# Sliding-window attention in sixteen fixed rounds: TensorE's order written out by hand

## The chip, the cores and the metric

The kernel runs on one core of one Trainium2 chip. The metric is the device time of one launch in microseconds (us), median of several runs; lower is better.

## What the reference computes

Two layers over 512 tokens of width 1024, everything in float32. Layer 0 mixes tokens with a stick-breaking attention beside a gated recurrence; layer 1 ("the second mixer") is a sliding-window attention with 16 query heads that share 4 key-value heads, a learned sink and a relative bias. Both layers follow it with a convolutional gated feed-forward net and a gate on a per-layer embedding. Only the second mixer is touched by the change:

```python
def mixer_c(h, w_in, q_norm, k_norm, sinks, rel_bias, w_out):
    q, k, v = jnp.split(h @ w_in, [1024, 1280], axis=-1)
    q = rmsnorm(q.reshape(B, S, 16, 64), q_norm)
    k = rmsnorm(k.reshape(B, S, 4, 64), k_norm)
    ...
    # per block of 128 queries, against the 256 keys of its own and the previous block
    logits = einsum('bqhgd,bkhd->bhgqk', q, k) * 64 ** -0.5 + bias   # masked to the band
    m = max(max(logits), sink)
    e = exp(logits - m)
    w = e / (sum(e) + exp(sink - m))
    o = einsum('bhgqk,bkhd->bqhgd', w, v)
    return o.reshape(B, S, 1024) @ w_out
```

Behind the mixer comes `h = h + mixer_c(...)`, then the feed-forward net, then `h = h + sigmoid(rmsnorm(h) @ ple_gate) * (p @ ple_proj)`.

## The kernel before

**Arithmetic.** Activations lie transposed: a tile holds 128 features by 512 tokens. A large product takes each operand apart into a rounded high part and a remainder (`whi`, `wlo` for weights, `xhi`, `xlo` for activations), and `mm3` (L180) adds three matmuls of 512 columns. `weights` (L155) loads 128 x 1024 floats on SP's queue into one of two `wraw` buffers and gives chunks of 512 columns: ScalarE casts `whi` (L168), VectorE subtracts `wlo` (L169), seven buffers of each. `fm_steps` (L187) is one output tile of 128 features, two chunks of twelve matmuls into `psfm`, with a `yield` behind each chunk; `fm` (L198) runs it through. `lead` (L273) does two output tiles at once while their inputs still arrive. `tm` (L206) makes the value projection with tokens on the partitions (`pstm`). The attention itself is plain float32: scores, transposes and values are single matmuls of whole float32 operands; in the trace one such matmul of scores, values or norm is recorded as two passes, and a transpose as one.

**Staging of the second mixer.** `mixer_c` (L696) handles two heads at a time: `jt` counts eight pairs of query heads. Per `jt` it needs the projection of 128 query features (`project`, L718: `psfm`, then `y` on VectorE and its square `sqc` on ScalarE), its norm (`normed`, L727: a matmul `pn` with a block of ones, then Ln and Exp on ScalarE and the product `qn` on VectorE), and two units of attention, `n0` = 0 and 2, each of two query blocks. A unit is
- `scores` (L748): q times k into `pl` (four matmuls, the two heads on rows 0 to 63 and 64 to 127 of the array), bias and maximum on VectorE (L766), four Exp on ScalarE, the sum and reciprocal, and four scalings of `lg` on VectorE (L783);
- `values` (L786): transposes of `lg` into `pt` (six or eight), a copy to `wt` by ScalarE for one head and by VectorE for the other, and the products with `vt` into `poc` (six or eight matmuls, the two heads on columns 0 to 63 and 64 to 127).

After the second unit `split_tile` makes the output projection's input. At the end, `fill` (the `embed` of layer 1, L879, into `pspp`) computes the embedding term that the last stage needs; it doesn't depend on the mixer.

**Who sets the order.** No line of `mixer_c` fixes it: the framework takes the instructions in the order of the program as priorities, and puts on each engine's queue, one after another, the first one whose inputs and buffers it reckons to be there. So the order on TensorE mixes projections, scores, transposes and values, down to single matmuls. Once built, each engine's queue runs strictly in its order. PSUM has two buffers of two banks (tag `z`: `pl`, `pt`, `pstm`), two single banks `mm` (`psfm`, `pn`, `pspp`) and two single banks `hg` (`poc`).

Of the kernel before, what the change touches and what calls it, by code (L numbers as in the profile page):

```python
# [9 lines left out]
F32 = mybir.dt.float32  # L10
F32R = mybir.dt.float32r
U8 = mybir.dt.uint8
AF = mybir.ActivationFunctionType
ALU = mybir.AluOpType

P = 128
# [7 lines left out]
NT = T // P  # L24
# [11 lines left out]
V_KN = V_QN + 1  # L36
# [6 lines left out]
LEAD = (2, 2)  # L43
# [7 lines left out]
class Kern:  # L51
# [642 lines left out]
        return bias  # L694

    def mixer_c(self, st, bias, fill):  # L696
        nc, A = self.nc, self.A
        xs = st["xs"]
        W = A["w_c"]
        with ExitStack() as ctx:  # L700
            kp = self.pool("c_keep", 1, ctx=ctx)
            tp = self.pool("c_tmp", 2, ctx=ctx)
            first = self.lead([W[8], W[9]], st)
            pss = [t[:, a, :] for t in (self.zpair("pstm"), self.zpair("pstm")) for a in range(2)]
            tok = self.tm(A["w_cv"], xs, 256, pss)
            for _ in range(LEAD[0]):
                next(tok)
            self.norm(st, "hg")
            rstd = st["rstd"]
            for _ in range(LEAD[1]):  # L710
                next(tok)
            self.columns(st, "hg")
            sink = kp.tile([P, 16], F32, name="sink")
            nc.gpsimd.dma_start(out=sink, in_=A["sinks"].partition_broadcast(P))
            gq = kp.tile([P, 1], F32, name="gq")
            nc.vector.tensor_scalar(out=gq, in0=self.v(V_QN), scalar1=0.125, scalar2=None, op0=ALU.mult)

            def project(wi):  # L718

                ps = first.pop(0) if first else self.fm(W[wi], xs)  # L720
                y = tp.tile([P, T], F32, tag="y", name="y")
                nc.vector.tensor_tensor(out=y, in0=ps, in1=rstd, op=ALU.mult)
                sq = tp.tile([P, T], F32, tag="sqc", name="sqc")
                nc.scalar.activation(sq, y, AF.Square)
                return y, sq

            def normed(y, sq, gain, tag, bufs):  # L727

                pn = self.bank("pn")
                nc.tensor.matmul(pn, self.blk, sq, start=True, stop=True)  # L730
                self.act(SET_EL, sq, pn, AF.Ln, scale=1.0 / 64, bias=self.eps)
                self.act(SET_EL, sq, sq, AF.Exp, scale=-0.5)
                o = kp.tile([P, T], F32, tag=tag, name=tag, bufs=bufs)
                nc.vector.scalar_tensor_tensor(out=o, in0=y, scalar=gain, in1=sq, op0=ALU.mult, op1=ALU.mult)
                return o

            kn = [project(8 + i) for i in range(2)]
            kn = [normed(*x, self.v(V_KN), "kn", 2) for x in kn]
            vt = []
            for _ in tok:  # L740
                pass
            for i in range(NT):
                t = kp.tile([P, 256], F32, tag="vt", name="vt", bufs=4)
                nc.scalar.activation(t, pss[i][:, 0:256], AF.Identity, scale=st["rcol"][:, i:i + 1])
                vt.append(t)
            os_, qs, pos, pend = [], {}, {}, []

            def scores(jt, n0):  # L748

# [33 lines left out]
                        nc.vector.tensor_scalar(out=lg[a][:, i, :wid[i]], in0=lg[a][:, i, :wid[i]], scalar1=dn[:, c:c + 1], scalar2=None, op0=ALU.mult)  # L783
                return jt, n0, wid, lg

            def values(jt, n0, wid, lg):  # L786
                if n0 == 0:
                    pos[jt] = self.bank("poc", "hg")
                po = pos[jt]
                wts = []  # L790
                pts = self.zpair("pt").rearrange("p a (i k) -> p a i k", i=2)
                for a in range(2):
                    for i in range(2):
                        for b in range(wid[i] // P):
                            nc.tensor.transpose(out=pts[:, a, i, b * P:(b + 1) * P], in_=lg[a][:, i, b * P:(b + 1) * P], identity=self.ident)  # L795
                for a in range(2):
                    pt = pts[:, a, :, :]
                    wt = tp.tile([P, 2, 256], F32, tag="wt", name="wt", bufs=4)
                    cp = nc.vector.tensor_copy if a else nc.scalar.copy
                    if wid[0] == wid[1]:  # L800
                        cp(out=wt, in_=pt)
                    else:
                        for i in range(2):
                            cp(out=wt[:, i, :wid[i]], in_=pt[:, i, :wid[i]])
                    wts.append(wt)
                for i in range(2):
                    n = n0 + i
                    for b in range(wid[i] // P):
                        j = n + 1 - wid[i] // P + b
                        for a in range(2):  # L810
                            g = 2 * (jt // 4) + a
                            nc.tensor.matmul(po[a * 64:a * 64 + 64, n * P:(n + 1) * P], vt[j][:, g * 64:(g + 1) * 64],  # L812
                                             wts[a][:, i, b * P:(b + 1) * P], start=(n == 0), stop=False, skip_group_check=True)
                if n0 == 2:
                    self.dump_ps(f"oc{jt}", po, tp)
                    os_.append(self.split_tile(self.xa, po))

            two = [project(jt) for jt in range(2)]
            for jt in range(2):
                qs[jt] = normed(*two[jt], gq, "qn", 3)  # L820
            for jt in range(8):
                for n0 in (0, 2):
                    pend.append(scores(jt, n0))
                    if jt + 2 < 8:
                        if n0 == 0:
                            nxt = project(jt + 2)
                        else:
                            qs[jt + 2] = normed(*nxt, gq, "qn", 3)
                    if len(pend) > 2:
                        values(*pend.pop(0))  # L830
            for x in pend:
                values(*x)
            fill()
            return os_


# [42 lines left out]
    def embed(self, L, pp, pr):  # L879

        nc, A = self.nc, self.A
        pt = [(hi, lo) for _, hi, lo in self.weights(A["pT"][L], 2 * T)]
        for c0 in range(2):
            for d0, hi, lo in self.weights(A[f"w_pp{L}"][c0], 1024):
                for j in range(2):
                    ps = self.bank("pspp")
                    for k in range(2):
                        sl = slice(j * 256 + k * P, j * 256 + (k + 1) * P)
                        self.mm3(ps, (hi[:, sl], lo[:, sl]), pt[k], k == 0, k == 1)
                    o = pp.tile([P, T], F32, tag="pr", name="pr", bufs=KT)  # L890
                    nc.scalar.copy(out=o, in_=ps)
                    pr.append(o)

    def ple(self, L, st, nxt, pp, pr):
        nc, A = self.nc, self.A
        xs = st["xs"]
        with ExitStack() as ctx:
            tp = self.pool(f"p_tmp{L}", 2, ctx=ctx)
            if pr:
                first = self.lead(A[f"w_pg{L}"][0:2], st)  # L900
            else:
                first = []
                self.embed(L, pp, pr)
            self.norm(st)
            rstd = st["rstd"]
            for m in range(KT):
                end = nxt is None and m == KT - 1
                ch = list(self.weights(A[f"w_pg{L}"][m], DM)) if end else None
                for c in (slice(0, 256), slice(256, T)) if end else (slice(0, T),):
                    if end:  # L910
                        ps = self.bank("psfm")[:, c]
                        for k in range(KT):
                            s = slice(k % 4 * P, k % 4 * P + P)
                            self.mm3(ps, [w[:, s] for w in ch[k // 4][1:]], [x[:, c] for x in xs[k]], k == 0, k == KT - 1)
                    else:
                        ps = first.pop(0) if first else self.fm(A[f"w_pg{L}"][m], xs)
                    g = tp.tile([P, T], F32, tag="pg", name="pg")[:, c]
                    nc.vector.tensor_tensor(out=g, in0=ps, in1=rstd[:, c], op=ALU.mult)  # L918
                    self.act(SET_SG, g, g, AF.Sigmoid)
                    nc.vector.tensor_tensor(out=g, in0=g, in1=pr[m][:, c], op=ALU.mult)  # L920
                    nc.vector.tensor_tensor(out=self.h[m][:, c], in0=self.h[m][:, c], in1=g, op=ALU.add)
                    if nxt is None:
                        nc.sync.dma_start(out=A["out"][m * P:(m + 1) * P, c], in_=self.h[m][:, c])
                if nxt is not None:
                    self.feed(self.xb, m, V_MIX + 8, nxt)
# [118 lines left out]
```

## Time and profile before

| | |
|---|---|
| median of 3 runs | 1335.3 us (1330.41 to 1336.96) |
| the profiled execution's own time | 1332.75 us |
| its span, first to last instruction | 1330.9 us |
| busy share of the span: TensorE matmul, VectorE, ScalarE, GpSimd | 99%, 65%, 51%, 2% |
| mean granted TensorE clock | 0.996 of full speed |
| the second mixer from its third projection to the start of the output projection | 762.72 to 878.35 us of the span |

The busy share of TensorE overstates its work, because consecutive matmuls overlap in the records: the time that one takes from the next is read from start to start.

### The profile page before, as it was taken

To read this page: it belongs to the slowest core of one execution; us is meant where nothing else is said; L and a number is where in the kernel's file an instruction comes from. 1 tells how busy PE (TensorE), PEld (TensorE's weight loads), DVE (VectorE), ACT (ScalarE), POOL (GpSimd) and SP (SyncE) were. 2 spreads that over 40 slices of the span, in tenths; PEclk is the share of its full clock that TensorE was granted. 3 is DMA by queue.
4 is the path that set the end of the run, shared out by engine and by line. 5 is a ranking of instruction groups with operands and counts; after the bars stand their busy time and mean duration, and the time that the engine had idled before them with its cause. 6 is when DMAs were issued, how large, how long until landed. Compare 5 with 4: busy or idle time off the path is not lost.

```text
span 1330.9 us, 16861 instructions
## 1 busy us (share of the span) xinstructions
PE 1311.9 (99%) x6162; PEld 1057.5 (79%) x6162; DVE 861.7 (65%) x1609; ACT 684.7 (51%) x1224; POOL 23.1 (2%) x116
## 2 busy tenths in 40 slices
PE   9999999999999999999998999999999999999998
PEld 7787767788888888888887866678888888888887
DVE  6557876766777347775458377665777536776555
ACT  6566876845544234454355465654644324444341
POOL 2000000000000000000010000000000000000000
PEclk8999999999999999999999999999999999999999
DMA  6321111133332333232364210023332333332232
GB/s 203 112 64 49 58 40 47 48 95 95 96 98 88 99 111 95 95 92 87 93 158 124 95 49 32 22 91 95 96 96 88 100 101 106 96 96 87 89 110 79
DMA packets 37283, 118.95 MB, mean 89 GB/s; under 512 B 4432, under 2 KB 8832, under 8 KB 37200
## 3 DMA queue, kind: packets, MB, share of 16 engines
q1 hardware_dynamic: 35856, 114.31, 27.8%
q0 software_dynamic: 1200, 3.55, 1.3%
q8 instruction: 48, 0.79, 0.2%
q14 instruction: 35, 0.29, 0.1%
q10 hardware_dynamic: 144, 0.02, 0.0%
HBM read 115.37 MB, written 2.49 MB: 89 GB/s over the span
## 4 chain that ended last, share of the span: by engine, by line
PE 89%; DVE 4%; DMA 3%; ACT 2%; issue 1%; SPq 0%; ACTq 0%; DVEq 0%
PE psfm L183 25%; PE psfm L185 24%; PE psfm L184 24%; DMA wraw<-w_pg 2%; PE pl L760 2%; PE poc L812 2%; PE pstm L217 1%; PE pstm L218 1%; PE pstm L216 1%; PE pt L795 1%; PE poa L591 1%; DVE wlo L169 1%; ACT sl L71 1%; PE pn L730 1%; PE psz L574 1%
## 5 line engine op out<-in xcount | busy, mean ns | idle before, releaser
L168 ACT CAST whi<-wraw 128x512 fp32r<-128x512 f32 (+1 forms) x428 | 260.6, 612 | 425.4 <-PE psfm L184 324.8
L183 PE MATMUL psfm<-xhi,whi 128*128 128x512 f32 (+1 forms) x1200 | 472.0, 394 | 4.9 <-DVE pg L918 3.8
L184 PE MATMUL psfm<-xlo,whi 128*128 128x512 f32 (+1 forms) x1200 | 468.4, 391 | 0.8 <-DVE xlo L234 0.8
L185 PE MATMUL psfm<-xhi,wlo 128*128 128x512 f32 (+1 forms) x1200 | 468.6, 391 | 0.1
L169 DVE TENSOR_TENSOR wlo<-wraw,whi 128x512 fp32r<-128x512 f32 (+1 forms) x428 | 287.5, 676 | 175.9 <-ACT whi L168 155.2
L183 PEld LDWEIGHTS psfm<-xhi,whi 128*128 128x128 f32 x1200 | 226.6, 189 | 52.7 <-issue 5.5
L184 PEld LDWEIGHTS psfm<-xlo,whi 128*128 128x128 f32 x1200 | 226.6, 189 | 49.0 <-DVE xlo L234 2.1
L185 PEld LDWEIGHTS psfm<-xhi,wlo 128*128 128x128 f32 x1200 | 226.4, 189 | 47.9 <-issue 1.3
L185 PE MATMUL psfm<-ghi,wlo 128*128 128x512 f32 x352 | 137.0, 389 | 0.0
L184 PE MATMUL psfm<-glo,whi 128*128 128x512 f32 x352 | 137.0, 389 | 0.0
L183 PE MATMUL psfm<-ghi,whi 128*128 128x512 f32 x352 | 137.0, 389 | 0.0
L852 DVE TENSOR_TENSOR u<-psfm,rstd 128x512 f32<-128x512 f32 x88 | 60.7, 691 | 69.3 <-PE psfm L185 64.5
L856 DVE SCALAR_TENSOR_TENSOR cy<-u,vec,cy 128x512 f32<-128x512 f32 x88 | 66.0, 751 | 35.6 <-ACT cy L855 35.4
L855 ACT ACTIVATE cy<-u,vec 128x512 f32<-128x512 f32 x88 | 71.7, 816 | 33.4 <-DVE u L852 33.3
L184 PEld LDWEIGHTS psfm<-glo,whi 128*128 128x128 f32 x352 | 66.1, 188 | 13.8
L185 PEld LDWEIGHTS psfm<-ghi,wlo 128*128 128x128 f32 x352 | 66.1, 188 | 13.6
L183 PEld LDWEIGHTS psfm<-ghi,whi 128*128 128x128 f32 x352 | 66.1, 188 | 13.6
L289 DVE TENSOR_TENSOR h<-h,psfm 128x512 f32<-128x512 f32 x48 | 33.0, 687 | 59.9 <-PE psfm L185 59.9
L857 DVE SCALAR_TENSOR_TENSOR cy<-u,vec,cy 128x512 f32<-128x512 f32 x88 | 65.9, 751 | 2.9
L869 ACT CAST ghi<-cy 128x512 fp32r<-128x512 f32 x44 | 27.3, 621 | 39.6 <-DVE cy L866 39.6
L233 ACT ACTIVATE xhi<-h,gains 128x512 fp32r<-128x512 f32 x48 | 34.6, 723 | 19.5 <-DVE h L289 10.2
L234 DVE SCALAR_TENSOR_TENSOR xlo<-h,gains,xhi 128x512 fp32r<-128x512 f32 x48 | 36.3, 756 | 8.7 <-ACT xhi L233 8.4
(217 smaller groups left out, 1306.1 us busy)
## 6 DMA issues: line engine op xcount, KB each, us to landing
wraw<-w_up SPq DMA_DIRECT2D x88, 512.0 KB, 3.5
wraw<-w_dn SPq DMA_DIRECT2D x32, 512.0 KB, 3.6
wraw<-w_ab SPq DMA_DIRECT2D x18, 512.0 KB, 3.5
wraw<-w_pg SPq DMA_DIRECT2D x16, 512.0 KB, 3.6
wraw<-w_dn SPq DMA_DIRECT2D x32, 192.0 KB, 2.4
wraw<-w_c SPq DMA_DIRECT2D x10, 512.0 KB, 3.5
wraw<-w_abo SPq DMA_DIRECT2D x8, 512.0 KB, 3.5
wraw<-w_co SPq DMA_DIRECT2D x8, 512.0 KB, 3.5
```

Of the source, the lines that this page charges most:

```text
L168: nc.scalar.copy(out=hi[:, :d1 - d0], in_=r)
L169: nc.vector.tensor_tensor(out=lo[:, :d1 - d0], in0=r, in1=hi[:, :d1 - d0], op=ALU.subtract)
L183: t.matmul(ps, w[0], x[0], start=first, stop=False)
L184: t.matmul(ps, w[0], x[1], start=False, stop=False)
L185: t.matmul(ps, w[1], x[0], start=False, stop=last)
L233: nc.scalar.activation(hi, h, AF.Identity, scale=g)
L234: nc.vector.scalar_tensor_tensor(out=lo, in0=h, scalar=g, in1=hi, op0=ALU.mult, op1=ALU.subtract)
L289: self.nc.vector.tensor_tensor(out=self.h[m], in0=self.h[m], in1=ps, op=ALU.add)
L852: nc.vector.tensor_tensor(out=u[:, 2:], in0=ps, in1=rstd, op=ALU.mult)
L855: nc.scalar.activation(y, u[:, 2:], AF.Identity, scale=w[2], bias=w[3])
L856: nc.vector.scalar_tensor_tensor(out=y, in0=u[:, 1:T + 1], scalar=w[1], in1=y, op0=ALU.mult, op1=ALU.add)
L857: nc.vector.scalar_tensor_tensor(out=y, in0=u[:, 0:T], scalar=w[0], in1=y, op0=ALU.mult, op1=ALU.add)
```

## The change

TensorE's instructions of the second mixer are issued in the order of the program (`tc.manual_schedule` for that engine alone). The order of the other engines stays the framework's, and so does the place of TensorE instructions from outside the region among those of the region. The program's order is rewritten: `values` is cut into `turned` (transposes and copies) and `values` (products); the projections of `jt` 2 to 7 and the embedding become a generator `dense` that gives half a projection, or a quarter of the embedding, at a time: twelve matmuls either way. Sixteen rounds follow, one per unit `u`: scores of unit u, values of unit u - 3, one step of `dense`, in odd rounds from 3 to 13 the norm `pn` of the head pair whose scores open the next round, transposes of unit u - 2. The loads of `sinks` and the scaled gain `gq` move ahead of `lead`; the key norms move behind the first query projection. No matmul, copy or load is added or left out.

```diff
             first = self.lead([W[8], W[9]], st)
-            kn = [project(8 + i) for i in range(2)]
-            kn = [normed(*x, self.v(V_KN), "kn", 2) for x in kn]
...
-            for jt in range(8):
-                for n0 in (0, 2):
-                    pend.append(scores(jt, n0))
-                    if jt + 2 < 8:
-                        if n0 == 0:
-                            nxt = project(jt + 2)
-                        else:
-                            qs[jt + 2] = normed(*nxt, gq, "qn", 3)
-                    if len(pend) > 2:
-                        values(*pend.pop(0))
-            for x in pend:
-                values(*x)
-            fill()
+            def dense():
+                for jt in range(2, 8):
+                    steps = project(jt, got)
+                    next(steps)
+                    yield
+                    for _ in steps:
+                        pass
+                    yield
+                yield from fill()
+
+            with tc.manual_schedule(engines={mybir.EngineType.PE}):
...
+                for _ in project(0, got):
+                    pass
+                for i in range(2):
+                    kn[i] = normed(*got[8 + i], self.v(V_KN), "kn", 2)
+                for _ in project(1, got):
+                    pass
+                qs[0] = normed(*got[0], gq, "qn", 3)
+                d = dense()
+                next(d)
+                qs[1] = normed(*got[1], gq, "qn", 3)
+                scored, keyed = [], []
+                for u in range(16):
+                    scored.append(scores(u // 2, u % 2 * 2))
+                    if len(keyed):
+                        values(*keyed.pop(0))
+                    next(d, None)
+                    if u % 2 and 2 <= u // 2 + 1 < 8:
+                        qs[u // 2 + 1] = normed(*got[u // 2 + 1], gq, "qn", 3)
+                    if len(scored) > 2:
+                        keyed.append(turned(*scored.pop(0)))
+                for x in scored:
+                    next(d, None)
+                    keyed.append(turned(*x))
+                    if len(keyed) > 1:
+                        values(*keyed.pop(0))
+                for x in keyed:
+                    values(*x)
+                for _ in d:
+                    pass
```

`turned` holds the transposes and copies of the old `values` word for word; `embed` gains a `yield` behind each twelve matmuls, and layer 0 runs it through as before.

## Rows read from the trace of the kernel before

**Rows 1.** Windows: the mixer, two double rounds; busy us by engine, clock, DMA share, GB/s
```profile
762.72:878.35 115.63, 114.17 (x674) 76.84 (x673) 84.04 (x320) 72.50 (x224) 0.16 (x3) 1.00 0.12 38
810.21:824.61 14.40, 14.40 (x86) 9.90 (x85) 11.04 (x44) 8.71 (x28) 0.00 (x0) 1.00 0.07 29
824.61:839.01 14.40, 14.40 (x86) 9.91 (x85) 10.60 (x41) 8.61 (x28) 0.00 (x0) 1.00 0.11 38
```

**Rows 2.** Timeline of TensorE, part of a double round: start, us, instruction, count
```profile
810.21 0.81 PE L795 MATMUL pt<-cst,lg 128*128 128x128 f32 x6
810.95 0.70 PE L760 MATMUL pl<-kn,qn 64*128 64x256 f32 x2
811.58 0.43 PE L812 MATMUL poc<-wt,vt 128*64 128x128 f32 x2
811.94 0.70 PE L760 MATMUL pl<-kn,qn 64*128 64x256 f32 x4
812.57 0.87 PE L812 MATMUL poc<-wt,vt 128*64 128x128 f32 x10
813.37 0.70 PE L760 MATMUL pl<-kn,qn 64*128 64x256 f32 x2
814.00 1.13 PE L730 MATMUL pn<-sqc,cst 128*128 128x512 f32 x2
814.96 1.04 PE L795 MATMUL pt<-cst,lg 128*128 128x128 f32 x8
```

**Rows 3.** Timeline of TensorE: blocks that stand whole, and what follows them
```profile
793.20 0.50 PE L183 MATMUL psfm<-xhi,whi 128*128 128x512 f32 x1
...
796.06 0.82 PE L795 MATMUL pt<-cst,lg 128*128 128x128 f32 x6
...
797.79 1.13 PE L760 MATMUL pl<-kn,qn 64*128 64x256 f32 x6
798.85 0.44 PE L812 MATMUL poc<-wt,vt 128*64 128x128 f32 x4
...
801.88 0.93 PE L760 MATMUL pl<-kn,qn 64*128 64x128 f32 x8
802.74 0.50 PE L183 MATMUL psfm<-xhi,whi 128*128 128x512 f32 x1
```

**Rows 4.** Timeline of all engines: from a norm's matmul to the scores behind it
```profile
815.16 0.69 ACT L71 ACTIVATE sqc<-pn,eps 128x512 f32<-128x512 f32 x1 [2.82 <-PE pn L730]
815.88 0.63 ACT L71 ACTIVATE sqc<-sqc 128x512 f32<-128x512 f32 x1
816.55 0.75 DVE L734 SCALAR_TENSOR_TENSOR qn<-y,gq,sqc 128x512 f32<-128x512 f32 x1 [0.33 <-ACT sqc L71]
817.40 0.70 PE L760 MATMUL pl<-kn,qn 64*128 64x256 f32 x2
```

**Rows 5.** Groups by line and form, 810.21 to 839.01 us: busy us, mean ns
```profile
L71 ACT ACTIVATE lg<-lg,nm 128x256 f32<-128x256 f32 x12 | 5.9, 498 | 0.0
L801 DVE COPY wt<-pt 128x512 f32<-128x512 f32 x2 | 1.4, 682 | 0.0
```

**Rows 6.** Timeline of VectorE: one unit's softmax, first and last group
```profile
814.11 0.48 DVE L766 CUSTOM_DVE_ANT_0 lg<-pl,bias,sink 128x256 f32<-128x256 f32 x1 [1.26 <-PE pl L760]
...
821.02 1.14 DVE L783 TENSOR_SCALAR lg<-lg,dn 128x256 f32<-128x256 f32 x4
```

**Rows 7.** Timeline of TensorE at the stage before, around its longest pause
```profile
708.31 0.77 PE L183 MATMUL psfm<-xhi,whi 128*128 128x512 f32 x1 [3.84 <-DVE pg L918]
...
709.30 0.63 PE L185 MATMUL psfm<-xhi,wlo 128*128 128x512 f32 x1
709.73 0.63 PE L183 MATMUL psfm<-xhi,whi 128*128 128x512 f32 x1
...
711.81 0.39 PE L185 MATMUL psfm<-xhi,wlo 128*128 128x512 f32 x1
```

**Rows 8.** Windows: one microsecond behind that pause; the clock stands third from the end
```profile
709.00:710.00 1.00, 1.00 (x4) 0.81 (x3) 0.96 (x3) 0.62 (x2) 0.00 (x0) 0.50 0.01 0
```

More of the change, by code (lines that the diff above doesn't have):

```diff
@@ L696, in mixer_c @@
     def mixer_c(self, st, bias, fill):
-        nc, A = self.nc, self.A
+        nc, tc, A = self.nc, self.tc, self.A
         xs = st["xs"]
@@ L702, in mixer_c @@
             tp = self.pool("c_tmp", 2, ctx=ctx)
[L703 to L712, printed above, removed]
             sink = kp.tile([P, 16], F32, name="sink")
@@ L716, in mixer_c, with project @@
             nc.vector.tensor_scalar(out=gq, in0=self.v(V_QN), scalar1=0.125, scalar2=None, op0=ALU.mult)
-            def project(wi):
-                ps = first.pop(0) if first else self.fm(W[wi], xs)
+            def project(wi, out):
+                ps = first.pop(0) if first else (yield from self.fm_steps(W[wi], xs))
                 y = tp.tile([P, T], F32, tag="y", name="y")
@@ L724, in project @@
                 nc.scalar.activation(sq, y, AF.Square)
-                return y, sq
+                out[wi] = (y, sq)
             def normed(y, sq, gain, tag, bufs):
@@ L735, in normed @@
                 return o
-            kn = [project(8 + i) for i in range(2)]
-            kn = [normed(*x, self.v(V_KN), "kn", 2) for x in kn]
[L739 to L746, printed above, removed]
+            os_, qs, pos, got, kn, vt = [], {}, {}, {}, [None, None], []
             def scores(jt, n0):
@@ L784, in scores, with turned @@
                 return jt, n0, wid, lg
-            def values(jt, n0, wid, lg):
-                if n0 == 0:
-                    pos[jt] = self.bank("poc", "hg")
-                po = pos[jt]
+            def turned(jt, n0, wid, lg):
                 wts = []
@@ L805, in values @@
                     wts.append(wt)
+                return jt, n0, wid, wts
+            def values(jt, n0, wid, wts):
+                if n0 == 0:
+                    pos[jt] = self.bank("poc", "hg")
+                po = pos[jt]
                 for i in range(2):
@@ L816, in values @@
                     os_.append(self.split_tile(self.xa, po))
-            two = [project(jt) for jt in range(2)]
-            for jt in range(2):
-                qs[jt] = normed(*two[jt], gq, "qn", 3)
-            for jt in range(8):
-                for n0 in (0, 2):
-                    pend.append(scores(jt, n0))
-                    if jt + 2 < 8:
-                        if n0 == 0:
-                            nxt = project(jt + 2)
-                        else:
-                            qs[jt + 2] = normed(*nxt, gq, "qn", 3)
-                    if len(pend) > 2:
-                        values(*pend.pop(0))
@@ L831, in mixer_c @@
-            for x in pend:
-                values(*x)
-            fill()
+            def dense():
[7 more added lines that the diff above has]
+                yield from fill()
+            first = self.lead([W[8], W[9]], st)
+            with tc.manual_schedule(engines={mybir.EngineType.PE}):
+                pss = [t[:, a, :] for t in (self.zpair("pstm"), self.zpair("pstm")) for a in range(2)]
+                tok = self.tm(A["w_cv"], xs, 256, pss)
+                for _ in range(LEAD[0]):
+                    next(tok)
+                self.norm(st, "hg")
+                rstd = st["rstd"]
+                for _ in range(LEAD[1]):
+                    next(tok)
+                self.columns(st, "hg")
+                for i in range(2):
+                    for _ in project(8 + i, got):
+                        pass
+                for _ in tok:
+                    pass
+                for i in range(NT):
+                    t = kp.tile([P, 256], F32, tag="vt", name="vt", bufs=4)
+                    nc.scalar.activation(t, pss[i][:, 0:256], AF.Identity, scale=st["rcol"][:, i:i + 1])
+                    vt.append(t)
+                for _ in project(0, got):
+                    pass
+                for i in range(2):
+                    kn[i] = normed(*got[8 + i], self.v(V_KN), "kn", 2)
+                for _ in project(1, got):
+                    pass
+                qs[0] = normed(*got[0], gq, "qn", 3)
[20 more added lines that the diff above has]
+                for _ in d:
+                    pass
@@ L892, in embed @@
                     pr.append(o)
+                yield
     def ple(self, L, st, nxt, pp, pr):
@@ L902, in ple @@
                 first = []
-                self.embed(L, pp, pr)
+                for _ in self.embed(L, pp, pr):
+                    pass
             self.norm(st)
```

## The prediction, on record before the run

> **What bounds the kernel now.** I read the page's busy shares first, then the windows of the second mixer, then TensorE's timeline inside it. From the third projection's norms to the output projection the mixer takes 115.63 us, and TensorE is busy for 114.17 of them at full clock [rows 1]. So TensorE's queue is the bound: what counts is what each instruction takes from start to start, and whether a new order leaves the engine waiting. DMA is not in play: 7 to 12% of its time [rows 1].
>
> The steady pattern is a double round (both units of one head pair, one projection, one norm) of 14.40 us, twice in a row [rows 1]. Its timeline shows where the order costs something: the scores of one unit come in fragments of two, four and two records, with pieces of values between them [rows 2]. A fragment of two takes 0.63 us (810.95 to 811.58), and so does one of four (811.94 to 812.57): the two heads lie on different rows of the array and run together when they stand side by side, and a lone one gains nothing. A whole block of eight short and long records takes 0.86 us [rows 3]. The same holds for values: a lone pair of records takes 0.36 us (811.58 to 811.94), the ten others 0.80 [rows 2].
>
> VectorE is the second engine to watch: busy for 11.04 of 14.40 us [rows 1]. One unit's softmax needs 8.05 us, from its first maximum at 814.11 to the end of its last scaling at 822.16 [rows 6].
>
> **The change: what the blocks save.** I price every item as a whole block, and compare the sum with the 115.63 us.
> - Scores: 0.86 us for an early unit (801.88 to 802.74). No late unit stands whole; six records with one lone pair take 1.06 (797.79 to 798.85), four steps of two passes, and a whole block of eight is four steps too: 1.06 [rows 3].
> - Values: an early unit has twelve records, six steps side by side. Ten records with two lone ones are six steps as well and took 0.80 us [rows 2]. A late unit has eight steps, by proportion 1.07.
> - Transposes: six take 0.74 us with the turn to scores (810.21 to 810.95) [rows 2]; eight by proportion 0.99.
> - Twelve matmuls of a projection between other work: 2.86 us (793.20 to 796.06) [rows 3]. The embedding's quarters are of the same shape.
> - A norm's matmul: 0.96 us (814.00 to 814.96) [rows 2].
>
> Eight double rounds of scores, values and transposes: 8 x (0.86 + 1.06 + 0.80 + 1.07 + 0.74 + 0.99) = 44.2. Fifteen blocks of twelve: 42.9. Six norms: 5.8. Ahead of the rounds two norms and one block of twelve: 4.8. Together 97.7, so the blocks save 115.6 - 97.7 = 17.9 us. A double round with a projection would be 12.2 instead of 14.40.
>
> **What the fixed order adds: the norm in front of its scores.** In odd rounds the norm `pn` stands ahead of one block of transposes, and the next round opens with the scores that need its result. Today the distance from `pn`'s start to scores that follow `qn` is 3.40 us (814.00 to 817.40): Ln, Exp, the product, each on an engine that was waiting for it [rows 2, 4]. In that time TensorE did other things. In the new order it has 0.96 + 0.99 = 1.95 us of work and then stands: 1.45 us at the least, with everything of this round queued behind (scores, so also the next softmax, values, the projection).
>
> It will rarely be the least, because ScalarE has the Exps of the same round's own scores ahead of Ln in the program. From the end of the scores `pn` ends 0.80 + 2.86 + 0.96 = 4.6 us later. By then VectorE must have done four maxima (4 x 0.48 = 1.9 [rows 6]), and, where the unit before it is late, its scalings (1.14 [rows 6]) and its copy (0.68 [rows 5]); ScalarE then four Exps (4 x 0.50 = 2.0 [rows 5]). That is 5.7, with the small steps 6.0: 1.4 us behind `pn`, and the wait becomes 2.9. Bounds: 1.45 with free engines, 1.45 + 2.0 = 3.45 if all four Exps come first. VectorE's load [rows 1] speaks for the late case, so I take 2.9. Six times: 17.4 us (8.7 to 20.7).
>
> **The other waits.** Values need both copies of `wt`. After the transposes of an even round only a scores block of 1.06 us stands between; VectorE's copy takes 0.68, and some 0.3 go by for the last transpose's end and the hand-over (0.27 us is what its record lasts beyond the next start: 8 records in 1.04 [rows 2]). So nothing, or what VectorE is in the middle of, up to a set of scalings, 1.14 [rows 6]. I take 0.4 in eight rounds, 3.2 (0 to 9). In odd rounds the wait for the norm covers it.
>
> At the end no `dense` step is left in round 15 or behind it. The last unit's softmax takes up to 8.05 us [rows 6], and TensorE has values, transposes, transposes and values for it, 0.80 + 0.99 + 0.74 + 1.07 = 3.6. The output projection lies outside the region and may fill what is left, if it gets a PSUM buffer; VectorE has little else to do then. I take 2.5 (0 to 5).
>
> Ahead of the rounds four norms share two `mm` banks with two projections; one may wait for a Ln of 0.69 [rows 4]: 0.5 (0 to 2). What moves ahead of `lead`, one load on POOL's queue and one small VectorE instruction, is not needed before the first scores some 40 us later: nothing. SP's queue gets the same loads in the same order, with DMA at 7 to 12% to hide them [rows 1]: nothing. `wt`, `lg` and `y` keep their buffers, and in the new order each is free a round before it is needed.
>
> **The clock.** In the stage before, TensorE stood for 3.84 us, and then the granted clock was 0.50, the lower of its two levels [rows 7, 8]. Eight matmuls took 3.50 us from 708.31 to 711.81 [rows 7] instead of some 1.8: 1.7 us lost. The new waits are shorter than that one in most rounds; I count one such drop: 1.7 (0 to 10). The Trainium skill, "TensorE: Matmul & The Clock Gate", section "Why this matters for your kernels", says that idle gaps between bursts of matmuls bring the clock back to half. By that rule each of the six waits is a candidate, and the sum would be 8.5 us higher; by the row only a wait near 3.84 is.
>
> **Sum.** -17.9 + 17.4 + 3.2 + 2.5 + 0.5 + 1.7 = +7.4 us. Against the profiled execution's own 1332.75 (its span is 1330.9) that is 1340.2. The median of the runs shown lies 2.55 higher, so I forecast 1342.7.
>
> **Rivals.**
> - *The waits stay at their least* (faster). Ln, Exp and product run at once, the output projection fills the end: 8.7 + 0.8 + 0.3 against 17.9, -8.1 us, 1327.2. For it: ScalarE was idle in front of that Ln for 2.82 us [rows 4], so it can be free when `pn` ends. Against it: VectorE's load. Place: the scores that open rounds 4, 6, 8, 10, 12, 14. It decides where the mean wait there is under (17.9 - 6.2) / 6 = 1.95 us. Chance 0.22.
> - *VectorE sets the round* (no change). If VectorE can't be pressed beyond its 11.04 in 14.40 us, a double round stays at 14.40 whatever TensorE's order, and 6 x (14.40 - 12.2) = 13.2 of the 17.9 go into waits spread over all blocks, not only in front of scores. Left: -4.7 + 3.0 for end and start = -1.7, 1333.6. For it: waits of TensorE ended by VectorE everywhere; against it: VectorE has 3.4 us idle in each double round. Chance 0.20.
> - *The waits trip the clock* (slower still). If all six reach the length that made the clock fall, 6 x 1.7 = 10.2 in place of 1.7: +15.9 us, 1351.2. For it: the bound of 3.45 is near 3.84 [rows 7]; against it: the least is 1.45. Chance 0.16.
> - *My forecast*: waits near 2.9 us, one drop of the clock. Chance 0.42; its own range 1336 to 1349.
>
> **How the numbers follow.** Faster or slower by 0.5% (6.7 us) is about what a measurement of this kernel can tell from no change. The first rival is faster: 0.22. The second lies within, and so does about a third of my forecast's own range (below 1342): 0.20 + 0.14 = 0.34. The rest is slower: 0.28 + 0.16 = 0.44. The range, with about one in ten left out on either side, goes from the first rival's time to just beyond the third's: 1326 to 1352.
>
> **What the profile after would show.** Right: `pl` in blocks of eight records, `poc` in blocks of twelve and sixteen, a double round's blocks adding up to about 12.2 us, and in front of the `pl` that opens rounds 4 to 14 an idle time of TensorE of 2 to 3.5 us, released by `qn` on VectorE, with Ln behind the Exps on ScalarE. Wrong: idle below 2 us there (the first rival); idle mostly in front of `poc` and `pt`, released by `wt` or `lg` (the second); a granted clock of 0.5 in several stretches of the mixer (the third). The saving itself is wrong if blocks cost more than priced: a late unit's scores well over 1.06 us, or switches between kinds of block that I have not counted. The prediction also fails if matmuls of the output projection are put into the rounds and take PSUM from them.

## The result, and the profile after

| | before | after |
|---|---|---|
| median, lowest to highest | 1333.84 us (1330.41 to 1336.96, 4 runs) | 1348.41 us (1346.07 to 1349.74, 4 runs) |
| ratio to before, 95% interval | | 1.0107 [1.0085, 1.013] |
| profiled execution's own time; its span | 1332.75; 1330.9 us | 1349.74; 1347.8 us |

The change makes the kernel slower by 14.6 us by the medians, and by 17.0 us from one profiled execution to the other. The sums below are held against the 17.0, since their terms come from these two traces.

The page after: busy us of each engine, share of the span, instructions.
```profile
PE 1310.1 (97%) x6162; PEld 1060.3 (79%) x6162; DVE 863.4 (64%) x1609; ACT 684.6 (51%) x1224; POOL 22.8 (2%) x116
```
TensorE's busy share falls from 99% to 97%, and those 97% hide a second loss, which the windows of after show: the mixer from the larger part of its value projection to its last values, one double round, and some microseconds behind one wait (the clock stands third from the end).
```profile
743.93:898.74 154.81, 134.93 (x791) 98.95 (x790) 93.50 (x332) 81.51 (x241) 0.00 (x0) 0.93 0.13 42
799.48:816.38 16.90, 14.28 (x85) 10.43 (x84) 10.84 (x41) 8.60 (x27) 0.00 (x0) 0.90 0.08 31
791.00:792.00 1.00, 0.00 (x0) 0.00 (x0) 1.00 (x3) 1.00 (x3) 0.00 (x0) 1.00 0.00 0
...
793.00:794.00 1.00, 1.00 (x11) 0.70 (x9) 0.58 (x3) 0.00 (x0) 0.00 (x0) 0.64 0.00 0
794.00:795.00 1.00, 1.00 (x12) 0.88 (x10) 0.86 (x6) 0.00 (x0) 0.00 (x0) 0.50 0.40 135
```
A double round takes 16.9 us (the next one 16.87) instead of 14.40 [rows 1]: TensorE stands for 2.6 of them, and the granted clock, 1.00 before, is 0.90 over the stretch. A clock of 0.90 over 16.9 us is 16.9 x 0.10 = 1.7 us lost. It comes as one stretch at the lower of the two levels (0.50, 1.2 of 2.4 GHz), behind a microsecond in which TensorE had nothing to do (791 to 792). There are six such stretches of some 3.4 us, from 793.3, 810.3, 827.4, 844.5, 861.5 and 878.6 us on. The other three executions show a mean clock of 0.990 to 0.992 against 0.988 in this one, so they may have had fewer such stretches; only this one was traced.

TensorE's waits of after, 735 to 895 us, without two of 0.8 us behind the key norms' Ln: who was waited for, us in total, times, longest.
```profile
PE pl L741 <- DVE qn L724: 12.6, 6, 2.6
PE poc L797 <- DVE wt L783: 5.1, 7, 1.1
PE poc L797 <- ACT wt L783: 0.5, 1, 0.5
```
The six waits for `qn` are 2.06, 1.80, 1.80, 1.80, 2.56 and 2.54 us, 2.1 on average. The first of them on TensorE's timeline, with the fall of the clock behind it:
```profile
788.50 1.02 PE L720 MATMUL pn<-sqc,cst 128*128 128x512 f32 x2
789.35 1.04 PE L774 MATMUL pt<-cst,lg 128*128 128x128 f32 x8
792.45 0.93 PE L741 MATMUL pl<-kn,qn 64*128 64x128 f32 x8 [2.06 <-DVE qn L724]
793.30 1.98 PE L797 MATMUL poc<-wt,vt 128*64 128x128 f32 x16
795.21 0.80 PE L183 MATMUL psfm<-xhi,whi 128*128 128x512 f32 x1
795.80 0.63 PE L184 MATMUL psfm<-xlo,whi 128*128 128x512 f32 x1
796.23 0.61 PE L185 MATMUL psfm<-xhi,wlo 128*128 128x512 f32 x1
```
The order is the predicted one, and the blocks stand whole. The scores behind the wait still run at full speed (0.85 us), but sixteen records of values take 1.91 us (793.30 to 795.21) where they take 1.03 at full clock, and matmuls of the projection stand 0.43 apart, as in [rows 7].

What ScalarE and VectorE did in that wait:
```profile
788.81 0.49 ACT L71 ACTIVATE lg<-lg,nm 128x256 f32<-128x256 f32 x1
...
789.61 0.69 ACT L71 ACTIVATE sqc<-pn,eps 128x512 f32<-128x512 f32 x1
790.42 0.59 ACT L780 COPY wt<-pt 128x512 f32<-128x512 f32 x1
790.91 0.64 ACT L71 ACTIVATE sqc<-sqc 128x512 f32<-128x512 f32 x1
```
```profile
791.04 0.69 DVE L780 COPY wt<-pt 128x512 f32<-128x512 f32 x1
791.65 0.74 DVE L724 SCALAR_TENSOR_TENSOR qn<-y,gq,sqc 128x512 f32<-128x512 f32 x1
```
The last Exp of the softmax ends at 789.30, before the norm's second matmul does at 789.52, and Ln (789.61) starts at once. The forecast had it behind the Exps by 1.4 us. What lies in the way is one copy of `wt` between Ln and Exp. From `pn` to the scores it is 3.95 us (788.50 to 792.45), against 3.40 in [rows 2, 4]. In the next three waits a cast of `whi` stands in that place (3.69 us from `pn` to the scores). In the last two ScalarE is late after all: the Exps and a copy of `pr`, the embedding's result, hold Ln until 0.8 us behind `pn` (857.19 to 858.03), and the wait is 2.56 us.

In front of the values the wait is not all that a late copy costs:
```profile
799.48 1.14 PE L741 MATMUL pl<-kn,qn 64*128 64x256 f32 x8
800.56 0.43 PE L797 MATMUL poc<-wt,vt 128*64 128x128 f32 x2
801.81 0.98 PE L797 MATMUL poc<-wt,vt 128*64 128x128 f32 x10 [0.82 <-DVE wt L783]
802.72 0.50 PE L183 MATMUL psfm<-xhi,whi 128*128 128x512 f32 x1
```
One head's first pair of records runs alone ahead of the wait, and the ten others take 0.91 us. Scores and values together take 3.24 us where 1.06 + 0.80 were priced: 1.38 more, of which only 0.82 is counted as waiting.

### The profile page after: what moved, and what is told of

It is laid out like the page before. It is cut to its first block, busy times and chain, and to the rows that moved or that the text cites. A ratio compares the mean times of both kernels' runs of the same rounds, so it can differ in the third digit from the quotient of the medians.

```text
span 1347.8 us, 16859 instructions
## 1 busy us (share of the span) xinstructions
PE 1310.1 (97%) x6162; PEld 1060.3 (79%) x6162; DVE 863.4 (64%) x1609; ACT 684.6 (51%) x1224; POOL 22.8 (2%) x116
## 4 chain that ended last, share of the span: by engine, by line
PE 88%; DVE 6%; ACT 3%; DMA 2%; issue 1%; SPq 0%; DVEq 0%; ACTq 0%
PE psfm L183 25%; PE psfm L184 24%; PE psfm L185 24%; DMA wraw<-w_pg 2%; PE poc L797 1%; PE pstm L216 1%; PE pstm L217 1%; PE pstm L218 1%; ACT lg L71 1%; DVE wlo L169 1%; PE poa L591 1%; ACT sl L71 1%; DVE lg L764 1%; PE psz L574 1%; PE psl L441 1%
```

## The experiments

My theory after the result: the new order costs what it makes TensorE wait for, most of all for `qn`, and what the clock then loses; the blocks do save what they were priced at. Its rivals: VectorE sets a round, so that a wait that is taken away comes back in front of other blocks; or the saving itself is smaller than priced. All versions below compute the whole result; the one with pads has matmuls more, whose result nobody reads. The kernel before, run again beside each group of versions, took 1333.6 to 1334.8 us, so medians of different groups compare within about a microsecond.

### The norm one round earlier
```
-                    if u % 2 and 2 <= u // 2 + 1 < 8:
+                    if u % 2 == 0 and 2 <= u // 2 + 1 < 8:
```


> One edit on the changed kernel: each of the six norms of the rounds is issued one round earlier (even rounds 2 to 12 in place of odd rounds 3 to 13), at the same place in its round. Theory A (the waits of the scores for the product behind the norm, 12.6 us in six waits, and the six stretches at half clock behind them, 6 x 1.7 us, are the loss): both go, 1348.4 - 12.6 - 10.2 = about 1326 us, no half-clock stretch in the mixer. Theory B (VectorE sets the round, the wait in front of the scores is only where it shows): the idle time moves to the values and the transposes, 1343 to 1349 us. Theory C (the clock falls because of the mix of short matmuls, not because of the pauses): the waits go but the six stretches stay, about 1336 us.

1338.03 us (1335.05 to 1339.07), ratio to before 1.0029 [1.0016, 1.0042]: 10.4 us less than the change, between what a wait gone for good and a wait that comes back elsewhere would give. It is nearest to the third theory's 1336, but the trace rules that one out: the waits for `qn` are gone, and so are the half-clock stretches behind them. Its waits, the four longest lines, and a double round:
```profile
PE poc L797 <- DVE wt L783: 5.0, 7, 1.0
PE poc L797 <- DVE wt L780: 3.3, 6, 0.8
PE poc L797 <- ACT wt L783: 1.3, 1, 1.3
PE poc L797 <- ACT wt L780: 1.2, 2, 0.6
```
```profile
800.69:815.07 14.38, 12.99 (x85) 9.42 (x84) 10.63 (x41) 8.37 (x29) 0.00 (x0) 1.00 0.13 39
```
Part of what was won is lost again in front of the values, 10.8 us instead of 5.6: the wait for `qn` had covered the copies of `wt` behind the transposes of odd rounds. The double round is back at the length of before, 14.38 us against 14.40 [rows 1], which is what a limit by VectorE would give. One half-clock stretch is left in the mixer (788.8 to 792.3), behind waits of 1.31 and 0.41 us.

### The norm and the transposes earlier
```
                     if len(keyed):
                         values(*keyed.pop(0))
-                    next(d, None)
-                    if u % 2 and 2 <= u // 2 + 1 < 8:
-                        qs[u // 2 + 1] = normed(...)
                     if len(scored) > 2:
                         keyed.append(turned(*scored.pop(0)))
+                    next(d, None)
+                    if u % 2 == 0 and 2 <= u // 2 + 1 < 8:
+                        qs[u // 2 + 1] = normed(...)
```


> As the run before, and the transposes of a round move ahead of its block of twelve matmuls, so that the copies of wt have that block and the next scores for cover. Theory A with the smaller waits (5.6 us in front of the values) also real: about 5 us less than the run before, near 1321 us. Theory B: the transposes now come 2.9 us earlier after their softmax and wait for the scalings instead, no gain over the run before or a loss of up to 10 us.

**1320.35 us** (1319.4 to 1321.23), 0.9893 [0.9869, 0.9916]: faster than both kernels. Now half a projection stands between the transposes and the values that need their copies. Its waits, without two of 0.8 us behind the key norms' Ln, and a double round:
```profile
PE pt L774 <- DVE mx L747: 1.8, 1, 1.8
PE pl L741 <- DVE mx L747: 1.1, 2, 0.7
```
```profile
791.37:803.30 11.93, 11.93 (x87) 8.87 (x85) 10.07 (x40) 8.14 (x28) 0.00 (x0) 1.00 0.15 45
```
No wait for `qn` or `wt`, no half clock in the mixer, and a double round of 11.93 us (others 11.95 to 12.68, the two longest with a wait of 0.41 and of 0.68 for maxima) against the 12.2 that were priced and the 14.40 of [rows 1]. So both rivals fall: the saving is as priced, and VectorE, busy for 10.07 of 11.93 us, does not set the round. The double round of 14.38 in the run before was not VectorE's limit but a copy asked for too late.

### The transposes alone
```
+                    if len(scored) > 2:
+                        keyed.append(turned(*scored.pop(0)))
                     next(d, None)
                     if u % 2 and 2 <= u // 2 + 1 < 8:
                         qs[u // 2 + 1] = normed(...)
-                    if len(scored) > 2:
-                        keyed.append(turned(*scored.pop(0)))
```
So the norm of an odd round stands directly in front of the scores that need it.

> The changed kernel with only the transposes moved ahead of the block of twelve matmuls; the norm stays in odd rounds, and so now stands directly in front of the scores that need it. Theory A: the small waits in front of the values (5.6 us) go, but each of the six scores waits for the whole chain behind the norm, 3.40 - 0.96 = 2.4 us or a little more, instead of 2.1, and the half-clock stretches stay where the pause is long enough: 1343 to 1348 us. If the two moves simply add (moving the transposes was worth 17.7 us on top of the norm's move), it would be about 1331 us.

1347.68 us (1345.86 to 1349.27), 1.0095 [1.0081, 1.0109], no different from the change. The copies' waits are gone, but now nothing covers the norm (its waits, and the first of them on TensorE's timeline; the others are 2.2 to 3.45 us):
```profile
PE pl L741 <- DVE qn L724: 19.7, 6, 4.4
```
```profile
787.08 1.02 PE L720 MATMUL pn<-sqc,cst 128*128 128x512 f32 x2
792.53 1.65 PE L741 MATMUL pl<-kn,qn 64*128 64x128 f32 x8 [4.44 <-DVE qn L724]
```
The two moves don't add: alone they are worth 10.4 and 0.7 us, together 28.1. Each move alone uncovers a wait that the other takes away.

### Work in the wait for `qn`
```
+                    odd = u % 2 and 2 <= u // 2 + 1 < 8
...
+                    if odd:
+                        pad = self.bank("pad", "hg")
+                        for _ in range(8):
+                            nc.tensor.matmul(pad, self.nones, xs[0][0], start=True, stop=True)
```
behind the transposes of the six odd rounds with a norm, in the order of the change.

> The changed kernel with eight extra matmuls of 512 columns (their result is read by nobody) behind the transposes of the six odd rounds, where TensorE waited 2.1 us for the product; the waits stay, but the engine works in them. If the pauses make the clock fall: full clock through the mixer and 6 x 1.7 = 10 us less, about 1338 us. If the clock falls for what TensorE runs and not for the pause: half-clock stretches stay and the time is 1348 us or more.

1342.0 us (1341.1 to 1344.23), 1.0059 [1.0039, 1.0079]: 6.4 us faster than the change, with 48 matmuls more. TensorE's timeline, and a window from one `pn` to the next:
```profile
793.17 1.04 PE L774 MATMUL pt<-cst,lg 128*128 128x128 f32 x8
793.96 2.09 PE L858 MATMUL pad<-xhi,cstr 128*128 128x512 f32 x8
...
796.27 0.93 PE L741 MATMUL pl<-kn,qn 64*128 64x128 f32 x8 [0.21 <-DVE qn L724]
```
```profile
792.31:809.50 17.19, 16.22 (x104) 11.76 (x102) 11.84 (x45) 10.08 (x34) 0.00 (x0) 1.00 0.11 32
```
The pads take the place of the wait and add nothing to it: from the transposes to the scores it is 3.10 us here (793.17 to 796.27) and in the trace of the change (789.35 to 792.45), and in the other five rounds the two agree within 0.02 us. The clock stays at 1.00. So the fall of the clock is a cost of its own, caused by the pauses. By the granted clock it is 6 x 1.7 = 10.2 us; from start to start, from the values behind a wait to the end of the half projection, it is 9.4 (793.30 to 798.74, for one, is 5.44 us where 3.90 is due at full clock). All of it came back: from the first scores to the end of the last values it is 120.05 us instead of 129.49, 9.4 less. The medians show 6.4 of that, and the spans of the two profiled executions 5.6, because in the run with pads the key norms began 3.8 us later (759.03 against 755.23), behind a pause of the stage before of 6.32 us instead of 3.52, with a half-clock stretch of 6.8 us (708.9 to 715.7).

### The change without its fixed order
```
-            with tc.manual_schedule(engines={mybir.EngineType.PE}):
+            with ExitStack():
```
The same program, with TensorE's order left to the framework, as in the kernel before.

> The changed kernel without the fixed order: the same program, but TensorE's queue again left to the framework. If the fixed queue exposes the waits (theory A), the framework fills them with other matmuls: no pause over 1 us, full clock, fragments back, near the kernel before, 1330 to 1340 us. If the order of the program itself (norm just ahead of its scores, sixteen rounds) is to blame: still near 1348 us.

1329.45 us (1325.71 to 1332.64), 0.9959 [0.9944, 0.9974]. The same instructions cost 19 us less than in the fixed order: its longest wait in the mixer is 0.8 us, and the clock does not fall there. It fills waits with matmuls of the projection, and pays with fragments. It is also 4.8 us below the kernel before beside it (1334.22), so part of what the new program gains needs no fixed order. What the framework's order would make of the version with both moves was not run.

### Why whole blocks save: three orders of the same matmuls
All start from the version with norm and transposes earlier. First, inside a block of scores, head outside and query block inside:
```
-                for i in range(2):
-                    n, nk = n0 + i, wid[i]
-                    k0 = (n + 1) * P - nk
-                    for a in range(2):
+                for a in range(2):
+                    for i in range(2):
+                        n, nk = n0 + i, wid[i]
+                        k0 = (n + 1) * P - nk
```


> The best kernel so far (norm and transposes earlier, 1320.35 us) with one edit: the four score matmuls of a unit run head by head instead of the two heads of a block side by side. Same instructions, same blocks, VectorE and ScalarE unchanged. If the blocks save because two heads run together on different rows of the array: an early unit's scores take about 1.5 us instead of 0.86, a late one's 1.9 instead of 1.06, 8 x (0.64 + 0.84) = 11.8 us, 1332 us. If they save only by fewer changes between kinds of matmul: no change, 1320 us.

1319.6 us (1316.8 to 1322.17), 0.9885 [0.9867, 0.9903]: no change, and the blocks still take 0.86 and 1.07 us. So heads need not alternate to run together.

Second, scores and values cut by query block, both heads in each piece (`scores` calls its new argument behind the first query block):
```
-                    scored.append(scores(u // 2, u % 2 * 2))
-                    if len(keyed):
-                        values(*keyed.pop(0))
+                    x = keyed.pop(0) if keyed else None
+                    scored.append(scores(u // 2, u % 2 * 2, x and (lambda: values(*x, parts=(0,)))))
+                    if x:
+                        values(*x, parts=(1,))
```


> The version with norm and transposes earlier, but in 13 rounds the scores and the values alternate by query block: scores of the first, values of the first, scores of the second, values of the second. Both heads stay in each piece. Nothing is added or left out; there are 26 more changes of kind of work. If a change of kind costs by itself (about 0.18 us each, estimated from the gaps where a run of transposes, scores or values begins): about 1325. If only the number of heads in a piece counts: 1320, no change.

Third, from the version with the head outside, all values between the scores of head 0 and those of head 1, so that each piece of scores has one head:
```
-                    scored.append(scores(u // 2, u % 2 * 2))
-                    if len(keyed):
-                        values(*keyed.pop(0))
+                    x = keyed.pop(0) if keyed else None
+                    scored.append(scores(u // 2, u % 2 * 2, x and (lambda: values(*x))))
```

> The version with norm and transposes earlier, but in 13 rounds the scores of one head stand ahead of the values and those of the other behind them. Nothing is added or left out; there is one more change of kind in each of 13 rounds. If a lone head pays full price because the two halves of the array then do not run together: a pair of blocks that took 1.06 takes near twice that, one of 0.86 near 1.6, so about 0.85 us in each of 13 rounds, 1331. If only the change of kind costs: 1322 to 1323.

1321.72 us (1319.68 to 1322.19), 0.9905 [0.989, 0.992], and 1331.07 us (1327.62 to 1333.26), 0.9977 [0.9966, 0.9989]. TensorE's timelines of a round, first with whole blocks, then in two pieces, then with one head in a piece:
```profile
795.77 1.13 PE L741 MATMUL pl<-kn,qn 64*128 64x256 f32 x8
796.83 0.88 PE L797 MATMUL poc<-wt,vt 128*64 128x128 f32 x12
797.64 1.09 PE L774 MATMUL pt<-cst,lg 128*128 128x128 f32 x8
```
```profile
796.15 0.70 PE L741 MATMUL pl<-kn,qn 64*128 64x256 f32 x4
796.78 0.44 PE L799 MATMUL poc<-wt,vt 128*64 128x128 f32 x4
797.15 0.70 PE L741 MATMUL pl<-kn,qn 64*128 64x256 f32 x4
797.78 0.66 PE L799 MATMUL poc<-wt,vt 128*64 128x128 f32 x8
798.37 1.09 PE L776 MATMUL pt<-cst,lg 128*128 128x128 f32 x8
```
```profile
799.06 1.13 PE L741 MATMUL pl<-kn,qn 64*128 64x256 f32 x4
800.11 0.88 PE L799 MATMUL poc<-wt,vt 128*64 128x128 f32 x12
800.92 1.13 PE L741 MATMUL pl<-kn,qn 64*128 64x256 f32 x4
801.98 0.77 PE L776 MATMUL pt<-cst,lg 128*128 128x128 f32 x5
```
Whole, the scores take 1.06 us and the values 0.81. In two pieces the scores take 0.63 + 0.63 and the values 0.37 + 0.59: 0.35 us more for two more turns. Four records of one head take 1.05 us (799.06 to 800.11), as long as eight of both: two lone heads cost twice the block. Over 13 rounds that is 13 x 0.35 = 4.6 us for the pieces, and for the lone heads (1.05 in seven late rounds, 0.84 in six early ones) 12.4. Measured from the first scores to the end of the last values it is 2.1 and 11.0 us (101.12 and 109.95 against 98.99; by the medians 1.4 and 10.7). The whole blocks' 2.9 us of waits for maxima (1.8 + 1.1) are gone from both traces, since TensorE came later to them; with these the pieces cost 5.0 and 13.9, the second 1.5 more than the rows explain. So both costs are real; the larger one is a head that stands alone in its piece.

### Two attempts to take the last waits
The key norms before the first query projection, and then also no half projection in round 11, so that one is left for the end:
```
+                for i in range(2):
+                    kn[i] = normed(...)
                 for _ in project(0, got):
                     pass
...
-                    next(d, None)
+                    if u != 11:
+                        next(d, None)
```


> The best kernel so far with the two key norms ahead of the first query projection, as in the kernel before. Two waits of 0.78 us for a PSUM buffer behind a Ln should go: 1.6 us less, 1318.8 us. If the wait only moves to the projection behind them: no change.

> As the run before, and round 11 takes no step of the projections and the embedding, so that the four quarters of the embedding fall in rounds 12 to 15 and the last softmax has 2.9 us of cover. The wait of 1.8 us in front of the last transposes should go, 1317 us; if round 11 then waits for its softmax instead, no gain or up to 3 us more.

1322.25 us (1320.0 to 1325.48), 0.9907 [0.9892, 0.9922], and 1323.51 us (1321.76 to 1325.26), 0.9915 [0.9902, 0.9929]: no gain. In the first, the key norms' waits fell from 1.6 to 0.3 us, and the stretch ahead of the first scores became 1.5 us shorter, as expected (from the matmuls `psc`, in the midst of the value projection, to the first `pl` 24.62 instead of 26.14 us). But the clock fell late in the mixer (860.1 to 863.5), behind the wait in front of the last transposes, and the stretch from the first scores to the last values grew by 1.6 us (100.55 against 98.99). The same wait, at 1.84 us, had left the clock at 1.00 in the version with both moves. This run's wait and a window behind it, then a window behind the wait in that version:
```profile
PE pt L774 <- DVE mx L747: 1.9, 1, 1.9
861.00:862.00 1.00, 1.00 (x12) 1.00 (x10) 1.00 (x2) 1.00 (x5) 0.00 (x0) 0.50 0.00 0
```
```profile
862.00:863.00 1.00, 1.00 (x16) 0.83 (x15) 1.00 (x5) 0.73 (x4) 0.00 (x0) 1.00 0.00 0
```
So the length of a pause alone doesn't tell whether the clock falls; what else decides was not found out. Without the half projection of round 11 one wait for the maxima grew to 3.4 us, and the clock fell in it (835.9 to 842.7).

Ahead of the mixer the half-clock stretch is 3.4 us long in some traces and 6.8 in others. It goes with the pause there: 2.1 to 4.2 us in traces with the short one, 4.2 to 6.4 in those with the long one. No edit touches that stage, and yet its pause, and with it the start of the mixer (the first key norm at 753.50 to 759.03 us in the versions that share this order), differs by some microseconds from run to run; why was not looked into.

## Why the prediction was right in its direction and wrong in its case

The sign, the place of the six waits and the range held: 1348.4 us lies in 1326 to 1352, 5.7 above the forecast. But what happened is nearest to the third rival, the one with the least chance: short waits that trip the clock every time. That the time still lies in the forecast's own range (1336 to 1349) is in part luck: the waits for `qn` were put 4.8 us too high and the clock 8.5 too low. By the prediction's own signs, three of the six waits were under the 2 us that it named for its first rival, and the several stretches at a clock of 0.5 were its sign of the third. Term by term, in us, against the 17.0 between the two profiled executions:

| term | forecast | from the traces |
|---|---|---|
| blocks | -17.9 | -17.9 as priced, see below |
| waits for `qn` | +17.4 | +12.6 |
| values waiting for copies | +3.2 | +5.6 |
| the end | +2.5 | +2.3 |
| ahead of the rounds | +0.5 | +2.1 |
| clock | +1.7 | +10.2 |
| sum | +7.4 | +14.9 |

The end is the stretch from the last round's scores to the last values, 886.38 to 898.74 us, less 6.4 us of the mixer's own blocks and 16 matmuls of the output projection that filled in, 3.7. Ahead of the rounds it is 20.6 us (743.93 to 764.50) against 18.5 for the same work before.

The sum leaves 2.1 of the 17.0 us out. In six rounds the values with a late copy cost some 3.5 us beyond the waits counted (1.38 - 0.82 in most, as shown above). Against that, the clock's cost from start to start is 9.4 instead of 10.2, and a norm ahead of transposes takes 0.85 us instead of 0.96, 0.6 less in six. 3.5 - 0.8 - 0.6 is 2.1.

- **The blocks' prices held.** Scores 0.86 and 1.06, early values 0.81, a norm 0.95 ahead of the rounds and 0.85 in them, half a projection 2.82 to 2.95 where nothing waits; only a late unit's values were a little cheaper, 1.03 instead of 1.07. The version without the waits shows the saving whole: a double round of 11.93 to 12.68 against 12.2, the longest with a wait of 0.68. It ran 13.9 us below the kernel before beside it (1334.22); 17.9 less 2.1 ahead of the rounds and 2.9 for maxima would be 12.9.
- **The reason given for that saving was half wrong:** "the two heads lie on different rows of the array and run together when they stand side by side": they run together in any order inside a piece, as the first of the three orders shows; what a fragment must not do is hold one head alone. And each turn from scores or values to other work costs some 0.2 or 0.15 us, which the prices of whole blocks held without naming it. The Trainium skill, "TensorEngine Tiling (Array Packing)", section "Key Properties", says that going from one way of dividing the array to another empties TensorE first, and that separate tiles work independently; the rows agree with both (scores are 64*128, values 128*64, transposes 128*128) and add the price.
- **The waits for `qn` were over-sized, 2.1 us each instead of 2.9.** The step that failed is that Ln would start 1.4 us behind `pn`, held up by the Exps: in the first wait they end at 789.30, just in time, and so they do in the next three. In place of that a copy of `wt` cost 0.55 us there, and a cast of `whi` 0.29 in the next three. Only in the last two did the Exps and a copy hold Ln, for 0.8 us. Where the norm stands directly in front of its scores, in the run with the transposes alone, Ln does start behind the Exps, at 789.53 with `pn` done at 788.10, and with no transposes in between that wait becomes 4.4, and the six 3.3 on average.
- **The clock was the largest miss, and the step that failed is its condition:** "by the row only a wait near 3.84 is" a candidate. In the trace of the change all six waits, 1.80 to 2.56 us long, were followed by a stretch at the lower level. In [rows 7, 8] one pause lowered the clock, and I took its length as the condition; one row can't say that a shorter pause does not. Nor does every such pause: in the run with the transposes alone the clock fell with five of six waits and not behind one of 2.22, and a wait of 1.84 us in the version with both moves left it up. The pads show the cause: with work in the pause the clock stays up. The rule of the Trainium skill that the forecast weighed ("TensorE: Matmul & The Clock Gate", "Why this matters for your kernels") gave 8.5 us more than the sum, 1351.2. That section speaks of longer gaps than these six, so the forecast stretched it; that idle gaps bring the clock back to half is what the trace shows, and shows for these shorter ones too.
- **The first rival named 1.95 us as the mean wait that decides.** The mean was 2.1, so by its sum the waits alone would have given near a draw. They did not: the run with pads, which has the waits' length and no fall of the clock in the mixer, is 7.8 us above the kernel before beside it (1342.0 against 1334.22), because the copies and the work ahead of the rounds cost more than forecast too.
- **The second rival fell:** VectorE does not set the round, as the version with both moves shows.

## What to carry to other kernels

In a fixed order, write for each consumer which block lies between it and the last producer, and count that cover against the whole way through the other engines: `pn` to scores is 3.4 us and needs a half projection, not a block of transposes. When two producers are late, move both before you judge either; here one move alone gave 10.4 us or nothing, both gave 28. And price each wait of TensorE with the clock that it can lose behind it: here six waits of 2.1 us on average cost some 3.7 each, and another of 1.84 us cost no more than itself.

## What the runs showed of the hardware

- The granted clock fell to 0.50 for some 3.4 us, 1.7 us of work, behind each of six pauses of 1.80 to 2.56 us, and once behind waits of 1.31 and 0.41 us close together. In other versions it stayed at 1.00 behind pauses of 1.84 and 2.22 us. From start to start a fall cost 1.5 to 1.6 us. Eight matmuls in the pause, 2.09 us of work, kept it at 1.00 and cost nothing themselves.
- Four records of scores of one head took 1.05 us, eight of both heads 1.06, in whatever order the eight stood: the halves of the array ran fully side by side, as long as both had work in the same piece.
- A piece of scores costs 0.2 us and one of values 0.15 beyond their matmuls, while a projection behind transposes shows nothing of the kind: six transposes ahead of it take 0.63 us (791.37 to 792.00 in the version with both moves), and 0.74 ahead of scores (798.74 to 799.48 in the change).
